# Stick-breaking attention: the causal mask moved from a matrix product into the scan

## The chip, the cores and the metric

One Trainium2 chip, one core of it. The metric is the device time of one execution in microseconds (us), taken as the median of the runs; lower is better. Names: PE is TensorE (PEld its weight loads), ACT ScalarE, DVE VectorE, POOL GpSimd, SP SyncE, whose queue issues most DMAs. `L1651` is line 1651 of the kernel before.

## The reference

One layer of a decoder in float32: a half-step SwiGLU network, a mixer, and a second half-step network, on 1024 tokens of width 1024 with 16 meta tokens ahead of them. In the mixer one combined projection feeds two groups of heads: four HGRN2 heads (a gated linear recurrence) and eight stick-breaking heads of width 64. The change lies in the stick-breaking part:

```python
def block(args):                       # 128 queries of one head
    qblk, start = args
    qpos = start + jnp.arange(BLOCK, dtype=jnp.int32)
    z = jnp.einsum('bhqd,bhkd->bhqk', qblk, k) * scale
    allowed = (kpos[None, :] < qpos[:, None]) & valid[None, :]
    log_beta = jnp.where(allowed, jax.nn.log_sigmoid(z), -jnp.inf)
    log_keep = jnp.where(allowed, jax.nn.log_sigmoid(-z), 0.0)
    suffix = lax.cumsum(log_keep, axis=3, reverse=True) - log_keep
    w = jnp.exp(log_beta + suffix)
    return jnp.einsum('bhqk,bhkd->bhqd', w, v)
```

So a key s gets the weight sigmoid(z_s) times the product of sigmoid(-z_j) over the keys j after it and before the query. A query sees only the keys before its own: its own key and the later ones have weight 0 and leave the product alone.

## The kernel before, in words

Matrix products run in a rounded float32 format, each operand split into a high and a low part, so that one product of the model is three on PE (high by high, high by low, low by high). L257, L258 and L259 are these three for the projections ("proj"); they are most of what fills PE around the change. The order of the large stages is: first network, combined projection for the stick-breaking heads, then the stage of the change, in which the attention of all eight heads runs while the projections for the HGRN2 heads are worked off beside it, then HGRN2, the output projection and the second network.

**One block of scores** (`sb_scores`, L1629 to L1669). A block is 128 queries of one head against its `nk` = 16 + 128(b+1) keys, cut into one to three pieces of up to 456 keys. A piece is worked from the last keys to the first:

- PE: two products L1648 and L1649 make the scores `z` in PSUM (pool `pz`, two buffers). For the piece that holds the last 128 keys, a third product L1651 adds the mask: the identity in bfloat16 (`ident_b`) times a 128 by 128 tile `neg_b` that holds -1e30 from the query's own key on and 0 before it. There are 8 heads x 8 blocks, so 64 of these among 112 pieces.
- ACT: `keep` = sigmoid(-z) (L1654) and `sig` = sigmoid(z) (L1655). A masked key so gets keep 1 and sig 0. POOL sets one more column of `keep`, after the last key, to 1 (L1643).
- DVE: a scan over the keys from the last to the first (L1658) makes the running product of `keep` in place. It starts from 1.0, or in the later pieces from the column where the piece before stopped. Its second operand does nothing (`bypass`); it is `idle`, one column in PSUM that is read over and over.
- POOL: when the first keys are reached, `sig` is multiplied by the running product one key further on (L1664). This is the weight w.

Then PE turns the weights over in pieces of 128 by 128 (`flip`, L1503 and, for the meta tokens, L1557) into PSUM (pool `ptr`, two buffers), ACT and DVE split them (L1626, L1627), and PE multiplies them with the values (L1578, L1580, "oacc").

**What sets the order.** PE's order is written by hand: `braid` (L1705) takes one job after the other (two blocks of one head), puts the job's scores at its own place, its flips two jobs later and its value products three jobs later, and spreads steps of the projections among them by their summed estimates (`n * 0.84` for a piece of scores, 107 a flip, 240 a value step). None of these estimates is changed. The orders of the other engines come from a scheduler, by the program's dependencies.

**Set-up.** `masks_blank` and `masks_cut` (L120 to L144) run in the first 15 us on DVE and POOL; besides the masks for HGRN2 they make `ident_b` and `neg_b`. `idle` is made at L2190, just ahead of `braid`, in a PSUM bank that the projections leave free during the stage.

Of the kernel before, what the change touches and what calls it, by code (L numbers as in the profile page):

```python
# [11 lines left out]
F32 = mybir.dt.float32  # L12
F32R = mybir.dt.float32r
BF16 = mybir.dt.bfloat16
U8 = mybir.dt.uint8
AF = mybir.ActivationFunctionType
ALU = mybir.AluOpType
# [3 lines left out]
P = 128  # L21
# [8 lines left out]
CHUNKS = [(META + 512, 512), (0, 264), (264, 264)]  # L30
PIECES = [(0, 264), (264, 264), (528, 256), (784, 256)]
LEVELS = [1, 2, 4, 8, 16, 32, 64]
NEG = -1e30


def drain(gen):
# [13 lines left out]
class Block:  # L50
# [19 lines left out]
    def setup(self):  # L70
        nc, a = self.nc, self.a
        self.loads = []
        self.const = c = self.pool("const")
        c.tile([P, 240], F32, name="base")
        self.pool("edge", side="right").tile([P, 504], F32, name="edge")
        self.dram = self.pool("scratch", space=DRAM)

        self.ident = c.tile([P, P], F32, name="ident")
        nc.vector.memset(self.ident, 1.0)
        nc.gpsimd.affine_select(  # L80
            out=self.ident, in_=self.ident, pattern=[[-1, P]],
            compare_op=ALU.is_equal, fill=0.0, base=0, channel_multiplier=1,
        )
        self.ones_d = c.tile([P, P], F32, name="ones_d")
        nc.vector.memset(self.ones_d, 1.0 / D)
        self.eps = c.tile([P, 1], F32, name="eps")
        nc.vector.memset(self.eps, EPS)
        nc.scalar.activation(c.tile([P, 1], F32, name="root"), self.eps, AF.Sqrt)

        self.g1 = self.column(a["ffn1_norm"][0], KT, "g1")  # L90
        self.gm = self.column(a["mix_norm"][0], KT, "gm")
        self.g2 = self.column(a["ffn2_norm"][0], KT, "g2")
        self.og = self.column(a["hgrn_out_norm"][0], 4, "og")
        self.l0 = self.column(a["hgrn_lb_logits"][0], 4, "l0")
        self.l1 = self.column(a["hgrn_lb_logits"][1], 4, "l1")
        self.qg, self.kg, self.qg8 = (c.tile([P, 1], F32, name=x) for x in ("qg", "kg", "qg8"))
        for h in range(2):
            s = slice(64 * h, 64 * h + 64)
            self.loads.append((self.qg[s], a["sb_q_norm"].rearrange("a d -> d a")))
            self.loads.append((self.kg[s], a["sb_k_norm"].rearrange("a d -> d a")))  # L100
        self.mx, self.lb, self.lbc = (c.tile([P, 4], F32, name=x) for x in ("mx", "lb", "lbc"))
        self.ident_b, self.neg_b = (c.tile([P, P], BF16, name=x) for x in ("ident_b", "neg_b"))
        self.masks = c.tile([P, len(LEVELS), P], U8, name="masks")
        self.ss = c.tile([P, 9, 2], F32, name="ss_x")
        self.ng1 = c.tile([P, KT], F32, name="ng1")
        nc.scalar.dma_start(*self.loads.pop(0))
# [13 lines left out]
    def masks_blank(self, sd):  # L120
        nc = self.nc
        nc.vector.memset(sd, 1.0)
        nc.vector.tensor_copy(self.ident_b, self.ident)
        nc.vector.memset(self.neg_b, 0.0)

    def masks_cut(self, sd):
        nc = self.nc
        nc.gpsimd.affine_select(
            out=self.neg_b, in_=self.neg_b, pattern=[[-1, P]],
            compare_op=ALU.is_gt, fill=NEG, base=0, channel_multiplier=1,  # L130
        )
        for i, n in enumerate(LEVELS):
            nb = P // (2 * n)
            for h in range(2):
                v = sd[:, i, :].rearrange("s (b h r) -> s b h r", h=2, r=n)[:, :, h, :]
                at = n * (1 - h)
                nc.gpsimd.affine_select(
                    out=v, in_=v, pattern=[[-2 * n, nb], [0, n]],
                    compare_op=ALU.is_ge, fill=0.0, base=-at, channel_multiplier=1,
                )  # L140
                nc.gpsimd.affine_select(
                    out=v, in_=v, pattern=[[2 * n, nb], [0, n]],
                    compare_op=ALU.is_gt, fill=0.0, base=at + n, channel_multiplier=-1,
                )  # L144
# [1484 lines left out]
    def sb_scores(self, pool, qs, ks, b, sigs):  # L1629
        nc = self.nc  # L1630
        nk = META + P * (b + 1)
        pieces = -(-nk // 512)
        size = -(-nk // pieces)
        size += size % 2
        q = qs[:, b * P : (b + 1) * P]
        kept = []

        def piece(s0, n):
            last = s0 + n == nk
            if last:  # L1640
                keep = pool.tile([P, nk + 1], F32, tag="keep", name="keep", bufs=3)
                sig = pool.tile([P, nk], F32, tag="sig", name="sig", bufs=6)
                nc.gpsimd.memset(keep[:, nk : nk + 1], 1.0)  # L1643
                kept.append(keep)
                sigs.append(sig)
            keep, sig = kept[0], sigs[-1]
            z = self.pz.tile([P, n], F32, tag="z", name="z")
            nc.tensor.matmul(z, q, ks[0][:, s0 : s0 + n], start=True, stop=False)  # L1648
            nc.tensor.matmul(z, q, ks[1][:, s0 : s0 + n], start=False, stop=not last)  # L1649
            if last:  # L1650
                nc.tensor.matmul(  # L1651
                    z[:, n - P :], self.ident_b, self.neg_b, start=False, stop=True
                )
            nc.scalar.activation(keep[:, s0 : s0 + n], z, AF.Sigmoid, scale=-1.0)  # L1654
            nc.scalar.activation(sig[:, s0 : s0 + n], z, AF.Sigmoid)  # L1655
            first, end = max(s0, 1), nk + 1 if last else s0 + n
            kv = keep[:, first:end][:, ::-1]
            nc.vector.tensor_tensor_scan(  # L1658
                out=kv, data0=kv, data1=self.idle.broadcast_to([P, end - first]),
                initial=1.0 if last else keep[:, end : end + 1],  # L1660
                op0=ALU.mult, op1=ALU.bypass,
            )
            if s0 == 0:
                nc.gpsimd.tensor_mul(sig, sig, keep[:, 1 : nk + 1])  # L1664

        return [
            (n * 0.84, lambda s0=s0, n=n: piece(s0, n))
            for s0 in reversed(range(0, nk, size)) for n in [min(size, nk - s0)]
        ]  # L1669
# [115 lines left out]
    def run(self):  # L1785
        nc, tc, a = self.nc, self.tc, self.a
# [11 lines left out]
        n = 512  # L1798
# [8 lines left out]
        with ExitStack() as c0:  # L1807
            with ExitStack() as c1:
# [8 lines left out]
                with tc.manual_schedule(engines={nc.tensor.engine}), ExitStack() as c2:  # L1817
# [87 lines left out]
                    first, hooks, steps_ahead = 32, 54, 58  # L1905
                    begin, finish = self.meta_in(marks)
# [19 lines left out]
                with tc.manual_schedule(engines={nc.tensor.engine}), ExitStack() as c2:  # L1926
# [200 lines left out]
                    last = norms[2]  # L2127
# [50 lines left out]
                with tc.manual_schedule(engines={nc.tensor.engine}):  # L2178
# [7 lines left out]
                    with ExitStack() as c2:  # L2186
                        self.att.append(self.pool("att1", ctx=c2))
                        tag = self.proj_tags[0]
                        self.proj_tags = [self.proj_tags[1]] * 2
                        self.idle = self.pproj.tile([P, 1], F32, tag=tag, name="idle", bufs=1)  # L2190
                        nc.vector.memset(self.idle, 0.0)
                        self.braid(jobs, islice(columns, 76), 1.22, 2.0, 3.0)
                    cf.close()
                    self.proj_tags[0] = tag
# [207 lines left out]
```

## Time and profile before

| | us |
|---|---|
| median of 3 runs | 1961.46 |
| the three runs | 1961.43, 1961.46, 1961.83 |
| the profiled execution, its own time | 1963.76 |
| its span, which the trace covers | 1962.1 |
| PE busy over the span | 1925.3 (98%) |
| DVE, ACT, POOL busy | 1387.2, 849.9, 449.7 |

The stage of the change stands in the trace from about 860 us, where the first piece of scores starts, to about 1124 us, where the last scan starts. In rows of the timeline the columns are the start in us, the duration in us, engine, line, operation, tiles, size and count; in brackets the idle time before it and what ended it. A matmul's duration covers its passage through the array, so products that follow each other overlap, and what one costs is read from start to start.

### The profile page before, as it was taken

What the parts mean: (1) busy time and instruction counts of PE and PEld (TensorE: products, weight loads), DVE (VectorE), ACT (ScalarE), POOL (GpSimd) and SP (SyncE); (2) the same over time, 40 slices, a digit from 0 to 9 for tenths busy, and PEclk for the clock granted to TensorE, in tenths of its full rate; (3) what the DMA queues carried; (4) which work ended last, traced back from release to release, by engine and by line L of the source; (5) the groups of instructions that cost most, each with busy time, mean ns of one, the idle gap of its engine ahead of it and who ended that gap; (6) DMA issues with size and microseconds to landing.
All of it is one profiled execution on the core that took longest, in us unless ns stands there. A gap on an engine that the chain in (4) does not pass through costs nothing.

```text
span 1962.1 us, 30371 instructions
## 1 busy us (share of the span) xinstructions
PE 1925.3 (98%) x10671; PEld 1616.6 (82%) x10671; DVE 1387.2 (71%) x2185; ACT 849.9 (43%) x1711; POOL 449.7 (23%) x626
## 2 busy tenths in 40 slices
PE   7999999999999999999999999999999999999999
PEld 6888888787888888888888978887888888888887
DVE  6977877877678665467777766667567777767774
ACT  6523443334444544356666635433132332344443
POOL 3010100001000003133333332210544645530000
PEclk9999999999999999999999999999999999999999
DMA  7356887757965415865454178655545444469473
GB/s 212 93 158 177 253 272 241 232 205 284 378 219 188 130 51 144 193 171 148 130 139 127 57 249 221 167 204 183 194 117 145 122 137 119 134 237 328 147 232 113
DMA packets 381687, 355.54 MB, mean 181 GB/s; under 512 B 129040, under 2 KB 284560, under 8 KB 381536
## 3 DMA queue, kind: packets, MB, share of 16 engines
q1 hardware_dynamic: 359728, 288.98, 48.9%
q0 software_dynamic: 20768, 64.63, 9.6%
q8 instruction: 84, 1.38, 0.3%
q14 instruction: 67, 0.55, 0.1%
q10 hardware_dynamic: 1040, 0.00, 0.0%
HBM read 237.95 MB, written 115.57 MB: 180 GB/s over the span
## 4 chain that ended last, share of the span: by engine, by line
PE 88%; DVE 4%; DMA 4%; ACT 1%; issue 1%; SPq 1%; POOL 1%; DVEq 0%; ACTq 0%; POOLq 0%
PE o L740 21%; PE qb L458 18%; PE qa L458 12%; PE qc L458 12%; PE proj L257 4%; PE proj L259 4%; PE proj L258 4%; PE flip L1503 2%; PE wo L258 1%; PE wo L259 1%; PE wo L257 1%; PE mq L1009 1%; PE oacc L1578 1%; PE oacc L1580 1%; PE z L1648 1%
## 5 line engine op out<-in xcount | busy, mean ns | idle before, releaser
L458 PE MATMUL qb<-T,wh 128*128 128x512 f32 x1056 | 344.5, 390 | 1.3 <-ACT T L317 0.8
L458 PEld LDWEIGHTS qb<-T,wh 128*128 128x128 f32 x1056 | 198.1, 188 | 46.3 <-issue 2.5
L458 PE MATMUL qa<-B,wh 128*128 128x512 f32 x696 | 226.7, 390 | 0.1
L257 PE MATMUL proj<-xh,wh 128*128 128x512 f32 (+2 forms) x640 | 213.4, 333 | 2.4 <-ACT st L1150 1.3
L740 PE MATMUL o<-t,w 128*128 128x512 f32 x924 | 212.3, 390 | 0.8 <-DVE u L551 0.7
L259 PE MATMUL proj<-xl,wh 128*128 128x512 f32 (+2 forms) x640 | 209.7, 328 | 0.8 <-DVE xl L1968 0.8
L258 PE MATMUL proj<-xh,wl 128*128 128x512 f32 (+2 forms) x640 | 209.6, 328 | 0.0
L740 PE MATMUL o<-parts 128*128 128x512 f32 x924 | 209.6, 389 | 0.0
L458 PE MATMUL qb<-T,wl 128*128 128x512 f32 x528 | 205.5, 389 | 0.0
L740 PEld LDWEIGHTS o<-t,w 128*128 128x128 f32 x924 | 172.7, 188 | 38.4 <-ACT sgm L989 1.1
L740 PEld LDWEIGHTS o<-parts 128*128 128x128 f32 x924 | 173.5, 188 | 36.0
L370 DVE TENSOR_TENSOR wl<-s,wh 128x512 fp32r<-128x512 f32 x160 | 165.5, 1034 | 51.3 <-ACT wh L368 50.4
L368 ACT CAST wh<-s 128x512 fp32r<-128x512 f32 x160 | 99.3, 622 | 188.7 <-PE qb L458 142.4
L458 PEld LDWEIGHTS qa<-B,wh 128*128 128x128 f32 x696 | 130.5, 188 | 27.6 <-DVE B L844 0.5
L368 ACT CAST wh<-raw 128x512 fp32r<-128x512 f32 x120 | 74.5, 621 | 156.8 <-PE qc L458 111.5
L458 PE MATMUL qa<-B,wl 128*128 128x512 f32 x348 | 135.4, 389 | 0.0
L257 PEld LDWEIGHTS proj<-xh,wh 128*128 128x128 f32 x640 | 120.6, 188 | 14.3 <-ACT st L1150 1.8
L259 PEld LDWEIGHTS proj<-xl,wh 128*128 128x128 f32 x640 | 120.4, 188 | 12.1 <-DVE xl L1968 1.2
L258 PEld LDWEIGHTS proj<-xh,wl 128*128 128x128 f32 x640 | 120.5, 188 | 10.0
L458 PE MATMUL qc<-B,wh 128*128 128x512 f32 x352 | 115.2, 390 | 2.8 <-DVE u L551 2.7
L458 PE MATMUL qc<-T,wh 128*128 128x512 f32 x352 | 117.0, 394 | 0.0
L458 PEld LDWEIGHTS qb<-T,wl 128*128 128x128 f32 x528 | 99.1, 188 | 20.2
(397 smaller groups left out, 3839.0 us busy)
## 6 DMA issues: line engine op xcount, KB each, us to landing
raw<-in_ffn_w_in_dram SPq DMA_DIRECT2D x176, 256.0 KB, 4.0
raw<-in_ffn_w_out_dram SPq DMA_DIRECT2D x112, 256.0 KB, 4.6
w2in<-both SPq DMA_DIRECT2D x28, 512.0 KB, 3.4
raw<-in_w_in_dram SPq DMA_DIRECT2D x25, 512.0 KB, 5.4
ks<-kD SPq DMA_DIRECT2D x32, 260.0 KB, 5.2
wout<-both SPq DMA_DIRECT2D x16, 512.0 KB, 3.7
wh<-w2in SPq DMA_DIRECT2D x27, 256.0 KB, 3.2
wl<-w2in SPq DMA_DIRECT2D x27, 256.0 KB, 3.1
```

Source lines behind the costliest of these rows:

```text
L257: nc.tensor.matmul(ps, wh[:, s], xs, start=k == 0, stop=False)
L258: nc.tensor.matmul(ps, wl[:, s], xs, start=False, stop=False)
L259: nc.tensor.matmul(ps, wh[:, s], xl[:, k, c0 : c0 + n], start=False, stop=k == nk - 1)
L368: nc.scalar.copy(hi, src)
L370: self.block_lo = nc.vector.tensor_sub(lo, src, hi.bitcast(F32))
L458: nc.tensor.matmul(ps, a[:, k, :], b[:, k, :], start=start and k == 0 and i == 0, stop=k == 3 and i == 2, skip_group_check=True,)
L740: nc.tensor.matmul(banks[bank][m], y[:, m * P : (m + 1) * P], z, start=start and at == 0 and e == 0, stop=q == nq - 1 and e == 2, skip_gro ...
L1009: nc.tensor.matmul(ps[at : at + 32, :], self.xm[:, 4 * h + k, :], got[i, h][:, k, :], start=h == 0 and k == 0, stop=h == 1 and k == 3, til ...
L1503: self.nc.tensor.transpose(ps[:m, j, :], src[:, s0 : s0 + m], self.ident)
L1578: nc.tensor.matmul(o[:, c], vj, w[0], start=j == 0, stop=False, skip_group_check=True)
L1580: nc.tensor.matmul(o[:64, c], vj[:, :64], w[1], start=False, stop=end, skip_group_check=True)
L1648: nc.tensor.matmul(z, q, ks[0][:, s0 : s0 + n], start=True, stop=False)
```

## The change

The mask product goes, and with it `ident_b`, `neg_b` and what made them. The scan of a piece that holds the last 128 keys starts at 0 in place of 1. Its second operand becomes a tile `begin` (128 by 512, float32, in the PSUM bank that held `idle`), and its second operation a maximum. `begin` is 0 but for a 1 where the scan meets the query's own key: the product stays 0 over the masked keys, the maximum lifts it to 1 at the own key, and from there on it is the same running product as before (a product of values between 0 and 1 is not changed by a maximum with 0). The later pieces read column 0 of `begin` over and over with `bypass`, as they read `idle`. `begin` is cleared and gets its ones (the identity read backwards) just ahead of `braid`. A pad in the constants grows by the 512 bytes a partition that the two tiles took, so that later tiles keep their places.

```diff
-        c.tile([P, 240], F32, name="base")
+        c.tile([P, 368], F32, name="base")
...
-        self.ident_b, self.neg_b = (c.tile([P, P], BF16, name=x) for x in ("ident_b", "neg_b"))
...
-        nc.vector.tensor_copy(self.ident_b, self.ident)
-        nc.vector.memset(self.neg_b, 0.0)
...
-        nc.gpsimd.affine_select(
-            out=self.neg_b, in_=self.neg_b, pattern=[[-1, P]],
-            compare_op=ALU.is_gt, fill=NEG, base=0, channel_multiplier=1,
-        )
...
-            nc.tensor.matmul(z, q, ks[1][:, s0 : s0 + n], start=False, stop=not last)
-            if last:
-                nc.tensor.matmul(
-                    z[:, n - P :], self.ident_b, self.neg_b, start=False, stop=True
-                )
+            nc.tensor.matmul(z, q, ks[1][:, s0 : s0 + n], start=False, stop=True)
...
-                out=kv, data0=kv, data1=self.idle.broadcast_to([P, end - first]),
-                initial=1.0 if last else keep[:, end : end + 1],
-                op0=ALU.mult, op1=ALU.bypass,
+                out=kv, data0=kv, data1=self.begin[:, : end - first] if last
+                else self.begin[:, :1].broadcast_to([P, end - first]),
+                initial=0.0 if last else keep[:, end : end + 1],
+                op0=ALU.mult, op1=ALU.max if last else ALU.bypass,
...
-                        self.idle = self.pproj.tile([P, 1], F32, tag=tag, name="idle", bufs=1)
-                        nc.vector.memset(self.idle, 0.0)
+                        self.begin = self.pproj.tile([P, 512], F32, tag=tag, name="begin", bufs=1)
+                        nc.vector.memset(self.begin, 0.0)
+                        nc.vector.tensor_copy(self.begin[:, 1 : P + 1], self.ident[:, ::-1])
```

On PE, at the first scores of the stage, before (in brackets the semaphores that an instruction waits for, named by the engine or queue that raises them):

```order
L1648 MATMUL z<-ks,qs 128x272
L1649 MATMUL z<-ks,qs 128x272
L1651 LDWEIGHTS ident_b
L1651 MATMUL z<-neg_b,ident_b 128x128
L1648 MATMUL z<-ks,qs 128x456 [waits PE_49,Activation_49]
L1649 MATMUL z<-ks,qs 128x456
```

and the same place after, with two more pieces:

```order
L1640 MATMUL z<-ks,qs 128x272
L1641 MATMUL z<-ks,qs 128x272
L1640 MATMUL z<-ks,qs 128x456 [waits Activation_49]
L1641 MATMUL z<-ks,qs 128x456
L1640 MATMUL z<-ks,qs 128x344 [waits Activation_49]
L1641 MATMUL z<-ks,qs 128x344
```

The weight load and the product of the mask are gone and nothing else has moved on PE; the wait for PE's own semaphore at the next score product has gone too. On DVE, where the stage begins, before:

```order
L1154 TENSOR_SCALAR st<-st,lbc 128x256 [waits DMAHW4_49,Activation_49]
L2191 MEMSET idle 128x1 [waits PE_49]
L1658 SCALAR_TENSOR_TENSOR keep<-keep,idle 128x144 [waits DVE_49,Activation_49,Pool_49]
L1658 SCALAR_TENSOR_TENSOR keep<-keep,idle 128x272 [waits Activation_49,Pool_49]
L1658 SCALAR_TENSOR_TENSOR keep<-keep,idle 128x457 [waits Activation_49,Pool_49]
```

and after (this listing calls the scan SCALAR_TENSOR_TENSOR, the trace TENSOR_TENSOR_SCAN):

```order
L1146 TENSOR_SCALAR st<-st,lbc 128x256 [waits DMAHW4_49,Activation_49]
L2180 MEMSET begin 128x512 [waits PE_49]
L2181 COPY begin<-ident 128x128 [waits DVE_49]
L1646 SCALAR_TENSOR_TENSOR keep<-keep,begin 128x144 [waits DVE_49,Activation_49,Pool_49]
L1646 SCALAR_TENSOR_TENSOR keep<-keep,begin 128x272 [waits Activation_49,Pool_49]
```

The clearing is wider, a copy is added, and the scans follow in the same order. In the first 35 us SP's queue changes as well: two weight loads (`raw`) move ahead of small loads of gains, since the scheduler finds DVE free earlier. Elsewhere the orders differ in one place, where SP issues a load of queries (`qs`) and a store (`hg_q`) that stood next to each other the other way round.

More of the change, by code (lines that the diff above doesn't have):

```diff
@@ L32 @@
 LEVELS = [1, 2, 4, 8, 16, 32, 64]
-NEG = -1e30
 def drain(gen):
```

## Prediction

> **What bounds the kernel now.** I read the page first: busy times, then the chain that ended last, by engine.
>
> ```profile
> PE 1925.3 (98%) x10671; PEld 1616.6 (82%) x10671; DVE 1387.2 (71%) x2185; ACT 849.9 (43%) x1711; POOL 449.7 (23%) x626
> PE 88%; DVE 4%; DMA 4%; ACT 1%; issue 1%; SPq 1%; POOL 1%; DVEq 0%; ACTq 0%; POOLq 0%
> ```
>
> PE holds 88% of the chain, so a product taken from PE is worth its place there unless the stage around it waits for something else. The busy times of the stage, 860 to 1124 us (the columns are length, then PE, PEld, DVE, ACT and POOL busy, the clock, the DMA share and GB/s):
>
> ```profile
> 860.00:1124.00 264.00, 257.11 (x1819) 228.30 (x1818) 192.18 (x309) 173.72 (x445) 94.13 (x137) 1.00 0.45 127
> ```
>
> PE is busy for 257 of 264 us at the full clock; DVE for 192. What PE waits for in this stage, and what the mask product makes others wait for, is in the list of waits (total, times, longest, in us):
>
> ```profile
> PEld flip L1503 <- issue: 8.0, 15, 0.9
> PEld z L1648 <- ACT sig L1655: 2.8, 6, 0.7
> PE flip L1503 <- DVE wu L1627: 2.7, 6, 0.7
> ACT keep L1654 <- PE z L1651: 6.8, 10, 3.0
> ```
>
> PE's gaps are short and few, most of them ahead of a flip that needs a PSUM buffer back from DVE. So the stage is PE's, with some fifteen places where ACT and DVE decide for a moment.
>
> **The change part by part.**
>
> The mask product. Its 64 instances are one group, of 230 ns each:
>
> ```profile
> L1651 PE MATMUL z<-neg_b,ident_b 128*128 128x128 bf16 x64 | 14.7, 230 | 0.0
> ```
>
> These 14.7 us are passage through the array and no price. The price is the start-to-start time with it and without it. With it, three places from the timeline of PE, followed by a value product, by a projection and by flips:
>
> ```profile
> 990.63 0.28 PE L1649 MATMUL z<-ks,qs 128*128 128x272 f32 x1
> 990.75 0.23 PE L1651 MATMUL z<-neg_b,ident_b 128*128 128x128 bf16 x1
> 990.79 0.36 PE L1578 MATMUL oacc<-wu,v 128*128 128x256 f32 x1
> 991.00 0.28 PE L1580 MATMUL oacc<-wu,v 128*64 128x256 f32 x1
> ...
> 986.11 0.27 PE L1649 MATMUL z<-ks,qs 128*128 128x144 f32 x1
> 986.22 0.23 PE L1651 MATMUL z<-neg_b,ident_b 128*128 128x128 bf16 x1
> 986.26 0.48 PE L257 MATMUL proj<-xh,wh 128*128 128x512 f32 x1
> 986.58 0.39 PE L258 MATMUL proj<-xh,wl 128*128 128x512 f32 x1
> ...
> 982.76 0.23 PE L1651 MATMUL z<-neg_b,ident_b 128*128 128x128 bf16 x1
> 982.83 0.61 PE L1503 MATMUL flip<-ident,sig 128*128 128x128 f32 x4
> ```
>
> Without it, from pieces that do not hold the last keys:
>
> ```profile
> 976.95 0.28 PE L1649 MATMUL z<-ks,qs 128*128 128x264 f32 x1
> 977.07 0.28 PE L1578 MATMUL oacc<-wm,v 128*128 128x256 f32 x1
> 977.19 0.28 PE L1580 MATMUL oacc<-wm,v 128*64 128x256 f32 x1
> ...
> 964.03 0.32 PE L1649 MATMUL z<-ks,qs 128*128 128x348 f32 x1
> 964.19 0.39 PE L257 MATMUL proj<-xh,wh 128*128 128x512 f32 x1
> 964.42 0.39 PE L258 MATMUL proj<-xh,wl 128*128 128x512 f32 x1
> ```
>
> The mask itself takes 0.04 us from its start to the next start (990.75 to 990.79, 986.22 to 986.26). But the product behind it takes longer: the value product 0.21 (990.79 to 991.00) in place of 0.12 (977.07 to 977.19), the projection 0.32 (986.26 to 986.58) in place of 0.23 (964.19 to 964.42). That is 0.09 more, and one mask costs 0.04 + 0.09 = 0.13 us; I take 0.125. Where flips follow, the rows show 0.07 to the first flip (982.76 to 982.83), and I take that alone. In the program's order a value product follows 26 masks, a projection 15, a flip 20, and the next score product 3. The last three stand where the stage begins and PE waits for ACT, and count as nothing. The sum on PE: 41 x 0.125 = 5.1, 20 x 0.07 = 1.4, together 6.5 us.
>
> [...]
>
> What of it lies on the path. PE's own waits swallow some. A flip waits for a buffer that was filled two flips earlier:
>
> ```profile
> 985.68 0.52 PE L1503 MATMUL flip<-ident,sig 128*128 128x128 f32 x3 [0.69 <-DVE wu L1627]
> ```
>
> The time of that release counts from earlier PE work, which comes earlier too; only masks that stood between that work and the waiting flip are lost. With 64 masks in 264 us, one in 4 us, and chains of 2 to 4 us, that is a half to one mask for each of the 15 waits in the list. I take ten masks of 0.1 us: 1.0 us lost (bounds 0.3 and 2.0). The score goes to ACT earlier by the mask's passage; ACT's idle time is no bottleneck, and I count nothing.
>
> The scan. It keeps its 112 instances. The rows give its rate with `bypass` and a start from a constant:
>
> ```profile
> 983.99 0.96 DVE L1658 TENSOR_TENSOR_SCAN keep<-keep,idle 128x393 f32<-128x393 f32 x1
> 987.74 0.43 DVE L1658 TENSOR_TENSOR_SCAN keep<-keep,idle 128x144 f32<-128x144 f32 x1
> ```
>
> (0.96 - 0.43) / 249 = 2.1 ns an element. No row has a maximum in the second place or a second operand that advances. The same instruction reads a second operand from PSUM already, one element a step, so I take no change. The bounds: nothing below, and half the rate more, 1.07 ns an element, above. For a head the 64 changed scans hold 144 + 272 + 400 + 265 + 329 + 393 + 457 + 345 = 2605 elements in eight pieces, 20840 in all, so that would be 22 us of DVE, priced as a rival below.
>
> [...]
>
> The making of `begin`. It stands on DVE ahead of the first scans:
>
> ```profile
> 1.05 0.17 DVE L85 MEMSET ones_d<- 128x128 f32 x1
> 1.36 0.81 DVE L122 MEMSET sd<- 128x896 f32 x1
> 6.09 0.27 DVE L123 CAST ident_b<-ident 128x128 bf16<-128x128 f32 x1
> 865.13 0.06 DVE L2191 MEMSET idle<- 128x1 f32 x1
> 865.32 5.13 DVE L1658 TENSOR_TENSOR_SCAN keep<-keep,idle 128x144 f32<-128x144 f32 x6
> 878.60 0.56 DVE L1627 TENSOR_TENSOR wu<-flip,wu 128x384 fp32r<-128x384 f32 x1 [1.87 <-ACT wu L1626]
> ```
>
> A clearing of 512 columns is an estimate of 0.17 + 384 x (0.81 - 0.17) / 768 = 0.49 us, the copy is near the cast of the same size, 0.27. Less the 0.06 that goes, the scans start 0.7 us later. Queued behind are six scans without a gap; POOL's weights wait for them, PE's flips for those. The delay is gone by 878.6, where DVE idles 1.87 us. In between PE has projections to do, and the first flips need scans that end more than a microsecond ahead of them. I take 0.3 lost, between 0 and 0.7.
>
> The set-up. The cast and the clearing go from DVE at 6.1 us, the select from POOL. PE's first product needs the first normalised row, which DVE makes behind this:
>
> ```profile
> 7.11 1.39 DVE L769 SCALAR_TENSOR_TENSOR junk<-row 128x1024 uint8<-128x1024 f32 x1 [0.66 <-DMA row<-in_x_dram]
> ```
>
> DVE waits there for the input, 0.66 us, so what goes ahead of it is worth nothing. The two weight loads that SP issues earlier serve products for which PE does not wait, and the exchanged pair in the stage, a load for the next head and a store, moves each by less than a microsecond. I count nothing for either, within 0.3 on both sides.
>
> The sum: -6.5 + 1.0 + 0.3 = -5.2 us. The profiled execution took 1963.76 (its span 1962.1), so it would take 1958.6. The median, 1961.46, lies 2.3 below it, and I move it by the same amount: 1956.3.
>
> **The rivals.**
>
> *More is swallowed.* If each of the waits eats a whole mask (2.0 lost), the start of the stage its full 0.7, and a mask with a flip behind it gives only the 0.04 of the others (20 x 0.03 = 0.6 less), -6.5 + 2.0 + 0.7 + 0.6 = -3.2 is left: 1958.3. For it speak the 15 waits, against it that DVE is idle for 72 of 264 us and so mostly waits for PE. 0.15.
>
> *The successor stays slow.* The 0.09 behind the mask may not be the mask's: the next weights may be late there for the short score products ahead (144 and 272 columns in the rows), and stay late. Then a mask gives its 0.04 alone, 64 x 0.04 = 2.6, plus the 0.6 at flips, less 1.3 for waits: 1.9, and 1959.6. Against it speak the rows without a mask, where behind 264 and 348 columns the successor keeps its pace. 0.07. [...]
>
> *The scan gets dearer.* If the maximum, or a second operand that advances in PSUM, costs 1.07 ns an element, DVE goes to 214 of 264 us and each changed scan of 144 to 457 elements takes 0.15 to 0.5 us longer, 0.34 on the mean (22 us / 64). PE loses this where a DVE chain decides, at some 20 places now (15 + 6 in the list of waits), each with about one scan ahead of it: 20 x 0.34 = 6.8. As DVE's load rises from 73% to 81%, I let as many places again join: 13.6 in all against the 5.2 gained, +8.4, 1969.9. It turns slower than before from 0.4 ns an element on. Against it speaks the scan's rate of 2.1 ns, which leaves time for a second operand. 0.06.
>
> *More is gained.* With the mask a wait of PE for its own semaphore goes too, ahead of those score products that reuse a buffer at once, and ACT gets scores earlier at the 10 places where it waited for the mask (6.8 us). If that shortens PE's waits by 1.5 us and nothing is swallowed, 6.5 + 1.5 = 8.0: 1953.5. 0.08.
>
> **How the numbers follow.** The forecast has 0.64: 1956.3, with its own range from 1955.0 to 1957.6 by the bounds of its terms (-6.5 with nothing swallowed, -3.8 with 2.0 and 0.7). What a measurement of this kernel can tell from no change is about 0.2%, 3.9 us: faster means under 1957.5, slower over 1965.4. Faster comes from the forecast (0.62 of its 0.64) and the larger gain (0.08): 0.70. Slower is the dear scan, 0.06. Within are the two smaller gains (0.22) and the forecast's edge (0.02): 0.24. The range runs from 1954.2 to 1959.8; it leaves out the far half of the larger gain and the dear scan.
>
> **What would show it.** In the profile after, the product behind each second score product should take its usual 0.12 or 0.23 us from start to start, and the group of the mask is gone. The stage from the first score product to the last scan should be 5 us shorter and the time up to 860 us the same to 0.5. Scans of 393 and 144 elements should still take 0.96 and 0.43 us, the clearing 0.5, the copy 0.3. I am wrong if the scans of the last keys get longer by over 0.1 us, if the product behind a score keeps its 0.21, or if PE's waits ahead of flips grow by more than 2 us in all.

## The result, and the profile after

| | before | after |
|---|---|---|
| median, us (21 runs each, taken side by side) | 1961.46 | 1958.08 |
| lowest and highest, us | 1959.79 to 1963.26 | 1955.34 to 1960.19 |
| ratio of the two, 95% interval | | 0.9982 [0.9975, 0.9988] |
| profiled execution, its own time, us | 1963.76 | 1959.65 |
| its span, us | 1962.1 | 1957.9 |

The change takes 3.4 us off (0.18%), where 5.2 were forecast. The median lies outside the forecast's own range (1955.0 to 1957.6) and inside the wide one, and the gain is just under the 0.2% from which the prediction calls a time faster: it gave faster 0.70, and what came, a smaller gain, 0.24. With 21 runs of each the interval of the ratio still lies wholly below 1. The page of the changed kernel, busy times and chain by engine:

```profile
PE 1919.8 (98%) x10607; PEld 1616.6 (83%) x10607; DVE 1390.4 (71%) x2184; ACT 849.6 (43%) x1711; POOL 450.5 (23%) x625
...
PE 89%; DVE 4%; DMA 3%; ACT 2%; issue 1%; POOL 1%; SPq 1%; DVEq 0%; ACTq 0%; POOLq 0%
```

PE has lost its 64 products (10671 to 10607) and 5.5 us of busy time, and it is still what the chain runs through. The stage, 860 to 1124 us, by busy times:

```profile
860.00:1124.00 264.00, 255.26 (x1774) 231.14 (x1773) 196.19 (x314) 175.33 (x449) 96.61 (x138) 0.99 0.45 126
```

PE is busy for 255.3 of the 264 us, where it was 257.1, DVE for 196.2 where it was 192.2, and the clock shows 0.99: three things to be explained below.

The product behind each score product does get its pace back. In the timeline of PE in the changed kernel a value product follows a score product of 400 columns, and a projection one of 392 and one of 144:

```profile
900.79 0.34 PE L1641 MATMUL z<-ks,qs 128*128 128x400 f32 x1
900.97 0.28 PE L1570 MATMUL oacc<-wu,v 128*128 128x256 f32 x1
901.09 0.28 PE L1572 MATMUL oacc<-wu,v 128*64 128x256 f32 x1
...
878.50 0.34 PE L1641 MATMUL z<-ks,qs 128*128 128x392 f32 x1
878.67 0.40 PE L249 MATMUL proj<-xh,wh 128*128 128x512 f32 x1
878.91 0.40 PE L250 MATMUL proj<-xh,wl 128*128 128x512 f32 x1
...
984.42 0.30 PE L1641 MATMUL z<-ks,qs 128*128 128x144 f32 x1
984.56 0.44 PE L249 MATMUL proj<-xh,wh 128*128 128x512 f32 x1
984.84 0.40 PE L250 MATMUL proj<-xh,wl 128*128 128x512 f32 x1
```

The value product starts 0.12 us before the next, the projection 0.24; those were the forecast values without a mask. Behind the short score product the projection still takes 0.28 here, and from the score's start it is 0.42 us (984.42 to 984.84) where it was 0.47 with the mask (986.11 to 986.58): this place gains 0.05 only. The eight places behind 144 columns gained 0.05 to 0.08 each. The scans are as long as before: 967 ns for 400 elements, 858 for 345, the rates forecast (rows below, in the first experiment).

**Where the gain went.** PE's order is the same in both kernels but for the masks, so the two timelines of PE can be laid side by side, product by product, and the lead of the changed kernel followed (the step at which it grows or shrinks belongs to one product). In the profiled pair:

| | us |
|---|---|
| lead when the first score starts, about 860 us | -2.0 |
| the 64 masks together (medians: -0.126 before 26 value products, -0.125 before 15 projections, -0.07 before 20 flips, 0 before 3 scores; some places less) | -6.2 |
| given back later in the stage, at 18 places of 0.05 to 0.29 | +2.1 |
| at the start of the stage: a wait | +0.3 |
| at the start of the stage: PE's clock at half | +1.5 |
| steps of under 0.1 besides | +0.4 |
| behind the stage | -0.2 |
| sum, the difference of the two spans | -4.1 |

The first row is not the change's. The kernel of the third experiment keeps the old set-up and led by 1.0 there in its profile; two more with the new set-up led by 1.5 and 0.4, and the seventh, which has it too, was 0.1 behind. So it varies from one execution to the next; why was not followed.

**The places that give back.** The list of waits in the stage of the changed kernel (total, times, longest, in us), for the flips and scores:

```profile
PEld flip L1495 <- issue: 8.9, 15, 1.0
...
PEld z L1640 <- ACT sig L1643: 3.9, 7, 0.8
PE flip L1495 <- DVE wu L1619: 3.6, 9, 0.8
...
PE flip L1495 <- DVE wm L1619: 1.8, 3, 0.6
```

Every one has grown: 8.0 to 8.9, 2.8 to 3.9, 2.7 to 3.6, and the last from 1.5. The rows of PE and of its weight loads (PEld) show largely the same waits from two sides, so they are not to be added. One place, before and after. Before, from a flip past a mask to the next flip that waits:

```profile
900.91 0.30 PE L1503 MATMUL flip<-ident,sig 128*128 128x128 f32 x1
...
901.65 0.23 PE L1651 MATMUL z<-neg_b,ident_b 128*128 128x128 bf16 x1
901.69 0.36 PE L1578 MATMUL oacc<-wu,v 128*128 128x256 f32 x1
901.89 0.28 PE L1580 MATMUL oacc<-wu,v 128*64 128x256 f32 x1
902.63 0.41 PE L1503 MATMUL flip<-ident,sig 128*128 128x128 f32 x2 [0.45 <-DVE wm L1627]
```

The same products after, without the mask:

```profile
900.23 0.30 PE L1495 MATMUL flip<-ident,sig 128*128 128x128 f32 x1
...
901.95 0.41 PE L1495 MATMUL flip<-ident,sig 128*128 128x128 f32 x2 [0.58 <-DVE wm L1619]
```

From flip to flip it is 1.72 us in both. The second flip waits for a PSUM buffer that DVE empties, and the work that leads to that began before the mask's place. The mask's 0.13 us turned into 0.13 us more of waiting, all of it.

A place need not wait beforehand to give a mask back. Here a score product follows a value product behind a mask, before:

```profile
896.26 0.23 PE L1580 MATMUL oacc<-wu,v 128*64 128x128 f32 x1
896.32 0.42 PE L1648 MATMUL z<-ks,qs 128*128 128x348 f32 x1
```

and after:

```profile
895.45 0.22 PE L1572 MATMUL oacc<-wu,v 128*64 128x128 f32 x1
895.64 0.43 PE L1640 MATMUL z<-ks,qs 128*128 128x348 f32 x1
```

The score product came 0.06 us behind, just in time for the buffer that ACT empties; now it comes 0.19 behind. And a long wait need not take anything: the flip at 985.68, which the prediction shows with 0.69 us of waiting, is the same after the change:

```profile
983.97 0.52 PE L1495 MATMUL flip<-ident,sig 128*128 128x128 f32 x3 [0.69 <-DVE wu L1619]
```

Its release came earlier by as much as PE did. So it is not the length of a wait that decides, but whether its release moves too.

DVE's larger share of the stage is not longer work: the stage is shorter, and the same 264 us hold a little more of it.

**The start of the stage.** Rows of PE, ACT and DVE in the changed kernel, in three fences. PE's score products wait for ACT, one of them 0.49 us:

```profile
862.04 0.29 PE L1640 MATMUL z<-ks,qs 128*128 128x272 f32 x1
...
866.08 0.43 PE L1640 MATMUL z<-ks,qs 128*128 128x348 f32 x1 [0.49 <-ACT sig L1643]
868.10 0.63 PE L250 MATMUL proj<-xh,wl 128*128 128x512 f32 x1
868.53 0.63 PE L251 MATMUL proj<-xl,wh 128*128 128x512 f32 x1
```

ACT waited for POOL, since `keep` has three buffers and the first comes free when POOL has made its first weights:

```profile
860.20 1.05 ACT L232 CAST wh<-raw 128x1024 fp32r<-128x1024 f32 x1 [3.14 <-DMA raw<-in_w_in_dram]
...
865.22 0.46 ACT L1642 ACTIVATE keep<-z 128x344 f32<-128x344 f32 x1 [0.27 <-POOL sig L1653]
```

And POOL waited for the first scan, which stands behind the making of `begin`:

```profile
861.28 1.22 DVE L234 TENSOR_TENSOR wl<-raw,wh 128x1024 fp32r<-128x1024 f32 x1 [3.79 <-ACT wh L232]
...
863.20 0.48 DVE L2180 MEMSET begin<- 128x512 f32 x1
863.72 0.29 DVE L2181 COPY begin<-ident 128x128 f32<-128x128 f32 x1
864.14 6.18 DVE L1646 TENSOR_TENSOR_SCAN keep<-keep,begin 128x144 f32<-128x144 f32 x7
```

Clearing and copy take 0.48 and 0.29 us, as estimated. Behind these waits PE's projections start 0.43 us apart (868.10 to 868.53) in place of 0.23. That is the clock; two stretches of the changed kernel's span (length, busy times of PE, PEld, DVE, ACT and POOL, granted clock, DMA share, GB/s):

```profile
862.00:867.30 5.30, 3.95 (x17) 2.25 (x17) 4.92 (x9) 4.71 (x13) 1.30 (x4) 1.00 0.55 152
867.30:870.70 3.40, 3.40 (x11) 2.72 (x10) 3.19 (x6) 1.44 (x5) 2.13 (x3) 0.50 1.01 205
```

and the first of them before, at the same work:

```profile
864.00:869.30 5.30, 4.42 (x22) 2.57 (x21) 5.05 (x9) 4.83 (x15) 1.80 (x5) 1.00 0.55 149
```

PE was busy for 3.95 of 5.3 us and then got half the clock for 3.4 us; with 4.42 of 5.3 before, it kept it. The granted clock is 1.00 in the first stretch and 0.50 in the second; what brings it down is not shown.

### The profile page after: what moved, and what is told of

Same layout as the page of the kernel before. It is cut to its first block, busy times and chain, and to the rows that moved or that the text cites. A ratio compares the mean times of both kernels' runs of the same rounds, so it can differ in the third digit from the quotient of the medians.

```text
span 1957.9 us, 30218 instructions
## 1 busy us (share of the span) xinstructions
PE 1919.8 (98%) x10607; PEld 1616.6 (83%) x10607; DVE 1390.4 (71%) x2184; ACT 849.6 (43%) x1711; POOL 450.5 (23%) x625
## 3 DMA queue, kind: packets, MB, share of 16 engines
q10 hardware_dynamic: 1040, 0.00, 0.0%
## 4 chain that ended last, share of the span: by engine, by line
PE 89%; DVE 4%; DMA 3%; ACT 2%; issue 1%; POOL 1%; SPq 1%; DVEq 0%; ACTq 0%; POOLq 0%
PE o L732 21%; PE qb L450 18%; PE qa L450 12%; PE qc L450 12%; PE proj L249 5%; PE proj L251 4%; PE proj L250 4%; PE flip L1495 2%; PE wo L250 1%; PE wo L249 1%; PE wo L251 1%; PE mq L1001 1%; PE oacc L1572 1%; PE oacc L1570 1%; DMA oT<-oD 1%
```

## The experiments

Nine runs, each beside runs of the kernel before on the same chip:

| kernel | median, us | before, us | ratio [95% interval] |
|---|---|---|---|
| 1 `begin` in SBUF, made in set-up | 1962.80 | 1961.72 | 1.0007 [0.9998, 1.0016] |
| 2 `begin` made, mask kept | 1962.28 | 1961.72 | 1.0002 [0.9993, 1.0011] |
| 3 mask left out, `begin` not made | 1958.48 | 1961.72 | 0.9982 [0.9974, 0.9991] |
| 4 two mask products | 1965.14 | 1961.72 | 1.0016 [1.0007, 1.0025] |
| 5 mask in rounded float32 | 1961.72 | 1961.47 | 1.0000 [0.9991, 1.0009] |
| 6 a third PSUM buffer for flips | 1997.05 | 1961.47 | 1.0182 [1.0168, 1.0196] |
| 7 `begin` cleared three times | 1961.39 | 1961.47 | 0.9999 [0.9991, 1.0008] |
| 8 `begin` cleared in two parts | 1958.91 | 1961.76 | 0.9986 [0.9977, 0.9995] |
| 9 the changed kernel again | 1957.86 | 1961.76 | 0.9982 [0.9973, 0.9991] |

**1. `begin` in SBUF, made in the set-up.** The changed kernel, edited:

```diff
-        self.pool("edge", side="right").tile([P, 504], F32, name="edge")
+        self.begin = self.pool("edge", side="right").tile([P, 504], F32, name="edge")
...
+        nc.vector.memset(self.begin, 0.0)
+        nc.vector.tensor_copy(self.begin[:, 1 : P + 1], self.ident[:, ::-1])
...
-                        self.begin = self.pproj.tile([P, 512], F32, tag=tag, name="begin", bufs=1)
-                        nc.vector.memset(self.begin, 0.0)
-                        nc.vector.tensor_copy(self.begin[:, 1 : P + 1], self.ident[:, ::-1])
```

> The changed kernel with begin in SBUF (the pad edge, 504 columns), made in the set-up where DVE idles, so that nothing stands ahead of the first scans of the stage. Theory: the making of begin costs 0.36 us through ACT's wait for a keep buffer, and the longer idling of PE brings the half clock of 1.4 us in some executions; both go, the 0.27 us wait of ACT for POOL at the start of the stage is gone, and the time is 0.4 to 0.7 us below the changed kernel, 1957.5. Rival: the place of begin in PSUM mattered, scans with two operands in SBUF take longer or hold up POOL, and the time is above the changed kernel by over 1 us with scans of 144 and 393 elements above 0.43 and 0.96 us.

The theory fell and the rival held: 1.1 us above the kernel before, where the changed kernel was 3.4 below. At the start of the stage ACT's wait for POOL and the half clock are gone, as expected (1.00 granted from 860 to 1124 us), but the scans did not stay as they were. Scans by shape, and POOL's longest product, in the changed kernel (busy in us, mean ns):

```profile
L1646 DVE TENSOR_TENSOR_SCAN keep<-keep,begin 128x400 f32<-128x400 f32 x8 | 7.7, 967 | 0.0
...
L1646 DVE TENSOR_TENSOR_SCAN keep<-keep,begin 128x345 f32<-128x345 f32 x8 | 6.9, 858 | 0.0
...
L1653 POOL TENSOR_TENSOR sig<-sig,keep 128x1040 f32<-128x1040 f32 x8 | 16.2, 2030 | 16.3 <-DVE keep L1646 11.6 <-ACT keep L1642 4.8
```

and with `begin` in SBUF (the tile is called `edge` there):

```profile
L1648 DVE TENSOR_TENSOR_SCAN keep<-keep,edge 128x400 f32<-128x400 f32 x8 | 15.9, 1987 | 0.0
...
L1648 DVE TENSOR_TENSOR_SCAN keep<-keep,edge 128x345 f32<-128x345 f32 x8 | 12.7, 1593 | 0.0
...
L1655 POOL TENSOR_TENSOR sig<-sig,keep 128x1040 f32<-128x1040 f32 x8 | 18.4, 2298 | 21.9 <-DVE keep L1648 21.9
```

967 became 1987 ns, 858 became 1593, and POOL's product went from 2030 to 2298. The place in SBUF is no cost by itself: the eight scans of 327 elements, beside which POOL makes no product in the trace of the changed kernel (the first runs from 878.62 to 879.51 there, POOL's next product from 879.68), take 885 ns as they do there, with both operands in SBUF:

```profile
L1648 DVE TENSOR_TENSOR_SCAN keep<-keep,edge 128x327 f32<-128x327 f32 x8 | 7.1, 885 | 0.0
```

In the changed kernel the eight scans of 400 elements do meet POOL's product of 1040 (901.93 to 902.90 and 901.67 to 903.70, for one). So the scans that meet POOL's product took 1987 ns with both operands in SBUF, where they took 967 with `begin` in PSUM, and the product 2298 in place of 2030; why is not shown. So the PSUM bank of `begin`, which the prediction passed over, is needed. The rival "the scan gets dearer" comes true in this version, but by another cause than its own, a cost of the maximum or of an operand that advances in PSUM.

**2. `begin` made, mask kept.** The kernel before, with the tile made and only its column 0 read:

```diff
-                out=kv, data0=kv, data1=self.idle.broadcast_to([P, end - first]),
+                out=kv, data0=kv, data1=self.idle[:, :1].broadcast_to([P, end - first]),
...
-                        self.idle = self.pproj.tile([P, 1], F32, tag=tag, name="idle", bufs=1)
+                        self.idle = self.pproj.tile([P, 512], F32, tag=tag, name="idle", bufs=1)
                         nc.vector.memset(self.idle, 0.0)
+                        nc.vector.tensor_copy(self.idle[:, 1 : P + 1], self.ident[:, ::-1])
```

> The kernel before, with the mask product, in which the tile of 512 columns is cleared and given its ones ahead of the stage but the scans read only its column 0, with bypass. It has the cost of making begin alone. Theory: ACT waits 0.3 us for a keep buffer at the start of the stage, +0.3 to +0.7 us, 1961.9, and PE's clock stays full more often than in the changed kernel, since the mask products still fill PE there. Rival: the making costs 1.5 us or more by itself (1963).

The median is 0.6 us higher, within the interval of no change; in the profile the start of the stage lost 0.16 us and nothing else moved. The making of `begin` is cheap.

**3. The mask left out, `begin` not made.** The kernel before without the third product:

```diff
-            nc.tensor.matmul(z, q, ks[1][:, s0 : s0 + n], start=False, stop=not last)
-            if last:
-                nc.tensor.matmul(
-                    z[:, n - P :], self.ident_b, self.neg_b, start=False, stop=True
-                )
+            nc.tensor.matmul(z, q, ks[1][:, s0 : s0 + n], start=False, stop=True)
```

> The kernel before without the mask product and with nothing in its place: the causal mask is left out of the computation. It has the gain on PE alone. Theory: the mask products free 6.2 us, waits ahead of flips swallow some 2.1, and -4.1 us is left, 1957.4; in the trace the product behind each second score product starts 0.13 us earlier, or 0.07 where it is a flip. Rival: waits swallow less and the making of begin was the larger loss; then it is -5 us or more, 1956.4.

It has the same ratio as the whole change, 0.9982; the median fell by 3.2 us, where 4.1 were expected. In the timeline of its profiled execution the masks gave 6.3 us and 18 places, 17 of them the same as in the changed kernel, took 2.0 back, with 0.07 lost at the start. So what is missing from the gain does not come from the scan or from `begin`. It is missing as soon as the product goes.

**4. Two mask products.** The kernel before with the product made twice:

```diff
-                nc.tensor.matmul(
-                    z[:, n - P :], self.ident_b, self.neg_b, start=False, stop=True
-                )
+                for i in range(2):
+                    nc.tensor.matmul(
+                        z[:, n - P :], self.ident_b, self.neg_b, start=False, stop=i == 1
+                    )
```

> The kernel before with the mask product issued twice (the masked scores get -2e30, with the same result). Theory: the 0.09 us at the successor is paid once for a change of the operand's type, and a second mask adds only its own passage, 0.05 to 0.06 us: 64 x 0.055 = 3.5 on PE, less what waits hide, +2.5 to +3.5 us, 1964.5. Rival: each mask product costs 0.13 us by itself (a weight load that is not pulled ahead): 64 x 0.13 = 8.3, +6 to +8 us, 1968.5.

Slower by 3.4 us. The place shown above, in this kernel:

```profile
902.03 0.29 PE L1652 MATMUL z<-neg_b,ident_b 128*128 128x128 bf16 x2
902.12 0.36 PE L1578 MATMUL oacc<-wu,v 128*128 128x256 f32 x1
902.33 0.28 PE L1580 MATMUL oacc<-wu,v 128*64 128x256 f32 x1
```

From the first mask to the end of its successor's slot it is 0.30 us with two, 0.24 with one (901.65 to 901.89), 0.12 without (900.97 to 901.09). Over all places a second mask costs 3.49 / 64 = 0.054 us, where the first costs 0.125. And the places that swallow work both ways: at 16 of the 18 that had given back in the changed kernel, or at the product next to them, 0.04 to 0.06 us were taken up, about one second mask each.

**5. The mask in rounded float32.** If the change of type from the score product to the mask and back costs the 0.09 behind it, a mask of the same type should not:

```diff
-        self.ident_b, self.neg_b = (c.tile([P, P], BF16, name=x) for x in ("ident_b", "neg_b"))
+        self.ident_b, self.neg_b = (c.tile([P, P], F32R, name=x) for x in ("ident_b", "neg_b"))
```

> The kernel before with the identity and the mask tile in the rounded float32 of the other products in place of bfloat16; the mask product stays. Theory: the 0.09 us at the successor is paid because the type of the operands changes there and the weights are not loaded ahead; without a change of type the mask takes one place in the row of short products, 0.06 to 0.12 us from start to start, and the successor keeps its 0.12 or 0.23, so the time is 0 to 3 us below the kernel before. Rival: any 128-column product between two others delays its successor; then the successor keeps its 0.21 or 0.32 and the time is that of the kernel before or more.

No difference in the time. The same place:

```profile
901.34 0.22 PE L1652 MATMUL z<-neg_b,ident_b 128*128 128x128 f32 x1
901.40 0.33 PE L1579 MATMUL oacc<-wu,v 128*128 128x256 f32 x1
901.57 0.28 PE L1581 MATMUL oacc<-wu,v 128*64 128x256 f32 x1
```

0.06 and 0.17 where bfloat16 has 0.04 and 0.20. The successor is still late by 0.05, and the sum, 0.23 against 0.24, is nearly the same. The type explains some 0.03 of the 0.08 us by which the successor is late; the rest comes with a product of 128 columns of either type at this place. In the profile before, the weights of the mask and of the value product behind it are both loaded from 901.65, the second load 0.04 us ahead of its product; in the changed kernel the value product's load starts 0.18 ahead (900.79 to 900.97). That this is the cause was not tried by itself.

**6. A third PSUM buffer for the flips.** The changed kernel, with two value sums as halves of one tile, so that a bank came free for every third flip:

```diff
+                return self.spare[: shape[0], : shape[1], :]
...
-                    acc.append(self.po.tile([P, 256], F32, tag="o", name="oacc"))
+                    acc.append(self.oa[:, self.accs % 2])
```

> The changed kernel with a third PSUM bank for flips in the stage: the two value sums share one bank, and every third flip goes to the bank set free. Theory: the 2.1 us that waits swallow are lost because a flip waits for one of two banks; with three the waits ahead of flips (8.9 us in the list) fall to 2 us or less, and the time is 3 to 6 us below the changed kernel, 1953.5. Rival: PE waits there for ACT's and DVE's work as such, which is late by as much with three banks; the waits move to the value products, and the time is within 1 us of the changed kernel.

36 us slower than before. Its list of waits shows that the experiment changed something else:

```profile
PEld oacc L1579 <- DVE ot L1621: 39.8, 28, 3.3
...
PEld flip L1503 <- issue: 0.3, 2, 0.2
```

The flips' waits are gone (8.9 to 0.3), but each value sum now waits for the readout of the sum before it, which shares its tile. What a third buffer would bring by itself stays open.

**7. `begin` cleared three times.** The changed kernel with a longer start on DVE:

```diff
-                        nc.vector.memset(self.begin, 0.0)
+                        for _ in range(3):
+                            nc.vector.memset(self.begin, 0.0)
```

> The changed kernel with the tile begin cleared three times in place of once, 1.0 us more on DVE ahead of the first scans. Theory: ACT's wait for the keep buffer grows by the 1.0 us, PE idles that much longer in the first 5 us of the stage, and PE's clock goes to half for 3.4 us in most executions and not in a quarter of them: +1 to +2.5 us over the changed kernel, 1960. Rival: projections cover the start of the stage, and nothing changes, 1958.

Slower than the changed kernel by 3.3 us, more than was expected; the whole gain is gone. In its profile PE waits 1.97 us and is granted half the clock for 6.8 us, twice the 3.4:

```profile
869.86 0.66 PE L1640 MATMUL z<-ks,qs 128*128 128x348 f32 x1 [1.97 <-ACT sig L1643]
```

```profile
868.60:875.40 6.80, 5.54 (x16) 4.59 (x17) 6.48 (x9) 3.62 (x10) 4.28 (x7) 0.50 0.82 170
```

The start of the stage lost 4.0 us for 1.3 us more on DVE: 1.7 where PE waits, and some 2.3 at products that run at half the clock. 10 of its 11 executions had a mean clock under 1.000.

**8 and 9. `begin` cleared in two parts, and the changed kernel again.** The eighth kernel clears only what the first scan reads, and the rest behind it:

```diff
-                        nc.vector.memset(self.begin, 0.0)
+                        nc.vector.memset(self.begin[:, :144], 0.0)
+                        self.uncleared = True
...
+            if self.uncleared:
+                nc.vector.memset(self.begin[:, 144:], 0.0)
+                self.uncleared = False
```

> The changed kernel, but only the first 144 columns of begin are cleared ahead of the first scan (an estimate of 0.18 us in place of 0.48), the other 368 behind it. Theory (the making of begin delays POOL's first product, that delays the third buffer of keep, PE idles 0.36 us longer, and in some executions that brings its clock to a half for 3.4 us): the wait of ACT for POOL's product, 0.27 us in the profile of the changed kernel, goes or falls under 0.1; the clock is below 1.000 in at most 1 of 11 executions, like the kernel before (4 of 54); the median is 0.2 to 0.6 us below the changed kernel's own, 1957.5 to 1957.9. Rival (the drops of the clock come with the mask's absence: PE runs faster ahead of the same idle stretch, whatever DVE does): still one execution in four below 1.000, and no difference in the median to 0.3.

> The changed kernel once more, unchanged, on the same chip as the one with begin cleared in two parts. Both theories: 1958.1, within 0.5 us, 3.4 us under the kernel before; the clock is below 1.000 in 2 to 4 of 11 executions, as it was in 5 of 21.

The ninth repeats the result: 3.9 us under the kernel before, where the first pair had 3.4. In the profile of the eighth ACT's wait for POOL is gone at this place and the start of the stage is 0.2 us quicker than before the change. Its median is not below the ninth's but 1.05 above, so the expected 0.2 to 0.6 us did not come out; the ratios' intervals overlap, and the two kernels are not told apart. Nor does the clock decide it: 2 of 11 executions under 1.000 against 3 of 11. In the profile of the ninth, whose mean is 0.999, the stage kept its clock:

```profile
862.50:867.80 5.30, 4.22 (x20) 2.51 (x19) 4.92 (x9) 4.78 (x14) 1.79 (x5) 1.00 0.69 186
...
1950.00:1955.30 5.30, 1.19 (x6) 0.65 (x4) 1.91 (x3) 0.00 (x0) 0.00 (x0) 0.80 0.51 198
```

The drop lies in the last 5 us, where PE has little left to do. So a mean under 1.000 does not say that the stage was hit, and how often it is stays open: in one of the two profiled executions of the changed kernel. What the two traces show to differ is when a transfer lands; that this decides is not shown. In the one that was hit ACT casts a weight at 860.20, after 3.14 us of waiting for its load, and PE starts its scores of 272 columns at 862.04. In the other the cast starts at 859.88 and those scores at 862.58. DVE's part of that weight stands ahead of `begin`, which so starts 1.16 us behind these scores in the one (862.04 to 863.20) and 0.31 in the other (862.58 to 862.89). In the second ACT never waits for POOL there.

## Why the prediction was right in kind and too high in size

*The masks: forecast -6.5, measured -6.2.* The price of 0.125 us, 0.04 at the mask and 0.09 at its successor, held for value products and projections, and 0.07 at flips. The fourth experiment shows that this is the price of a first mask: a second one behind it costs 0.054. The 0.3 that is missing is at places like the one behind 144 columns, where the price was lower.

*What waits swallow: forecast 1.0, measured 2.1; this is the term that was mis-sized.* The prediction counted the 15 waits ahead of flips in its list, took "ten masks of 0.1 us" for them, in the middle of its own bounds of 0.3 and 2.0, and put every other place at nothing. The runs showed 18 to 20 places with 0.11 to 0.12 on the mean: 2.1 in the profile after, 2.0 in the third experiment, 2.3 in the ninth, the last two with almost nothing else in the way. The 15 waits gave back 1.0, 0.8 and 1.0 of this, so that part was sized rightly in sum. It did not come from a part of a mask at each: in the third experiment six of the 15 took a whole mask, one took 0.05 us and eight took nothing, among them three of the four longest. The other 1.1 to 1.2 us went at eleven or twelve places that the forecast left out: score products, value products, projections, and flips outside the 15. In the profile before PE stood idle for 0.03 us or less at nine of the eleven in the profile after. It came there just in time, and began to wait when the mask ahead was gone. The mechanism was right, that a release which counts from earlier work is not brought forward by what goes behind that work; what failed is the count, since the list shows where PE waits already and not where it would wait if it came sooner.

The first rival had 2.0 for the waits, which is near what came, but its clause "each of the waits eats a whole mask" did not hold, and its two others, a dearer start and a smaller price at flips, did not happen in general. That its 1958.3 lies next to the measured 1958.08 is luck.

*The making of `begin`: forecast 0.3 (0 to 0.7).* Clearing and copy were sized rightly. The cost at the start was 0.16 in the second experiment, 0.07 in the ninth, 0.3 in the profile after. What the prediction did not have is the clock: in the profile after, 0.3 us more of waiting, on top of idle time that was there before, was followed by 3.4 us at half the clock, which cost another 1.5 us. It named the projections as cover; at that clock they started 0.43 us apart in place of 0.23.

*The scan: forecast no change.* Right: 967 and 858 ns for 400 and 345 elements, the same as before, with a maximum and an advancing second operand in PSUM; that is (967 - 858) / 55 = 2.0 ns an element, so the rate of 2.1 did leave time for that operand. The first experiment shows that the place of that operand was the risk, not the operation.

*The signs to be seen.* The successors' pace and the scans came as said. The time up to 860 us was to be the same to 0.5 us, and was 2.0 off, for a reason outside the change. The stage from the first score product to the last scan was to be 5 us shorter; it was 1.8 shorter in the profile after, with the half clock in it, 4.0 in the third experiment and 3.7 in the ninth. The waits ahead of flips were not to grow by more than 2 us in all. The rows of PE grew from 4.2 to 5.6, those of its weight loads from 8.4 to 9.4 (flips of the meta tokens included); they are the same waits seen twice, so this is 1.0 to 1.4 and the sign did not show, because over half of the loss lay elsewhere. The prediction adds such rows too, in the "15 + 6" of its dear scan.

Put together from the ninth run's profile: -6.3 + 2.3 + 0.1 + 0.1 = -3.8, and its median fell by 3.9. So close a match is partly chance, since a profile is one execution: the third experiment's gives -4.0 for the stage, and its median fell by 3.2.

## What to carry to other kernels

Before a gain on the busiest engine is summed, go through the places behind each removed piece one by one. A wait whose release does not come earlier takes the whole piece (0.13 us of 0.13 at the flip shown with 0.45 us of waiting); one whose release comes earlier by as much takes nothing, however long (0.69 us before and after). A place that is just on time becomes a wait (a start 0.06 us behind became 0.19), and no list of waits shows it. The price of a short product is read from start to start, over itself and its successor (0.04 and 0.09 us for the mask). Small work that is put at the head of a stage is judged by the buffers behind it and by the granted clock in the trace there, not by its own length: 0.77 us of work for `begin` was followed by a loss of 1.8 us in the profile after.

## What the runs showed of the hardware

- The clock dropped without a long idle stretch: in the profile after PE had been busy for 3.95 of 5.3 us, with no wait over 0.5, and was granted half for the next 3.4; with 4.22 of 5.3 (the ninth run) and 4.42 (before) it was not. These are single cases and no threshold.
- Scans with the second operand in SBUF took 1987 ns on the mean for 400 elements beside POOL's products, 967 with that operand in PSUM, and POOL's products of 1040 elements 2298 in place of 2030. Where no product of POOL ran, a scan of 327 elements took 885 ns both ways.
- A 128-column product between float32 products cost 0.125 us, 0.07 ahead of flips and 0.05 to 0.08 behind score products of 144 columns; a second one behind it cost 0.054. Its type hardly mattered (0.24 in bfloat16 against 0.23 at one place).
